# A second, modulated copy of the feed-forward operand in a row of 544 columns, read by 18 of 22 inner tiles

## The chip, the cores and the metric

The kernel runs on one core of one Trainium2 chip. The metric is the device time of one launch in microseconds (us). Times are medians over runs; one more execution is taken by the hardware profiler, and everything said below of single instructions is from that one.

## The reference

A two-layer diffusion backbone: 256 latent tokens `x` and 256 context tokens `y`, 1024 channels, 2816 inner channels in each feed-forward. Layer 0 mixes by differential attention, layer 1 by a Fourier transform; each mixer stands between two half-step SwiGLU feed-forwards. Every sub-layer normalizes, multiplies by a norm gain and a scale, and adds a shift.

```python
def modulate(h, shift, scale):
    return h * (1 + scale) + shift
def swiglu(h, w_gu, w_d):
    g, u = jnp.split(h @ w_gu, 2, axis=-1)
    return (jax.nn.silu(g) * u) @ w_d
...
x = x + 0.5 * mx[2] * swiglu(modulate(rms_norm(x, norm_g[i, 0]), mx[0], mx[1]), ffn1_w_gu[i], ffn1_w_d[i])
...   # attention (layer 0) or Fourier mixing (layer 1)
x = x + 0.5 * mx[8] * swiglu(modulate(rms_norm(x, norm_g[i, 2]), mx[6], mx[7]), ffn2_w_gu[i], ffn2_w_d[i])
```

The context tokens are needed only up to the attention of layer 0. So there is one feed-forward over 512 columns (layer 0, the first) and three over the 256 latent columns (layer 0 the second, layer 1 the first and the second). These three are called the **later feed-forwards** below, L0f1, L1f0 and L1f1.

## The kernel before, in words

**Products.** Everything is float32, and each product is made of three TensorE matmuls (`mm3`, L140): each operand is split into a rounded `hi` and a rest `lo`, and hi·hi, hi·lo and lo·hi are summed in PSUM. The first operand of a matmul (128 columns of weights) stays in the array, the second (256, 258 or 512 token columns of `xop_hi`, `xop_lo`) moves through it.

**Weights.** `unit` (L130) takes a weight tile of 1 MB by DMA from the SP queue into a ring of raw buffers and splits it in four pieces: ScalarE casts (`whi`, L101), VectorE subtracts (`wlo`, L102). In the later feed-forwards the rings of `whi` and `wlo` hold three tiles each (2 and 1 from `more_buffers`). So the cast of tile j + 3 can start only when the matmuls of tile j have ended.

**A later feed-forward.** `ffn` (L340) goes through the 22 inner tiles in two halves of 11. For each, `gate_up` (L301) runs 2 parts x 8 channel tiles x 3 = 48 matmuls into one PSUM tile `gu` out of a pool `psA` of **two**. So tile j + 2 can begin only when the evacuation of tile j has read its PSUM. The operand is not yet modulated: `scaled` (L294) writes x times the scale, without rstd (which is not known before the whole sum of squares is) and without the shift; the shift goes through the same weights as two extra columns (`scaled_shift`, L290), which makes 258. The evacuation puts both back: ScalarE copies the shift's product (`shw`, L317), VectorE multiplies both parts by rstd into `gus` (L319, which frees the PSUM tile), ScalarE takes Silu (L320), VectorE makes the product `hh` (L321), and `split` (L322) makes `h_hi` and `h_lo` of it. After each half, eight output tiles `dn` (`down`, L324) of 33 matmuls of 256 columns follow.

**Beside it.** The layers' scale, shift and gate vectors come from a large matrix by VectorE products with `junk` outputs (L197), `step(ROOM1)` (L347) placing some of them between the tiles, each with its own raw buffer and DMA. `modulated` (L280) makes an operand with rstd and shift in it: per channel tile VectorE `hmod` (L284), ScalarE `xop_hi` (L285) and VectorE `xop_lo` (L286). Before, only the attention uses it.

**Order.** Each engine works through its own list in order. The lists are made by the tile framework's scheduler, which places an operation when its modelled time and priority come up; `tc.high_priority(offset=URGENT)` moves an operation up by 200, `unit` moves weights up by `AHEAD = 60`.

Of the kernel before, what the change touches and what calls it, by code (L numbers as in the profile page):

```python
# [75 lines left out]
def tile_kernel(ctx: ExitStack, tc, xyT, small, rows, tables, w_mod0, w_mod, w_gu, w_d0, w_d, w_qkv, w_o, w_f, out):  # L76
# [196 lines left out]

    SX, SY = slice(0, NT), slice(NT, 2 * NT)

    gap(const, 416, "xop")
    xop_hi = const.tile([P, KT, 2 * NT], F32R, name="xop_hi")
    xop_lo = const.tile([P, KT, 2 * NT], F32R, name="xop_lo")

    def modulated(layer, w, s, r, dt):  # L280
        sl = (SX, SY)[s]
        h = work.tile([P, 512], F32, tag="hh", name="hmod")
        sh = mod[:, layer, s, 3 * w, dt:dt + 1]
        V.scalar_tensor_tensor(h[:, :NT], xy[:, dt, sl], amul[:, layer, s, w, dt:dt + 1], r, op0=ALU.mult, op1=ALU.mult)  # L284
        S.activation(xop_hi[:, dt, sl], h[:, :NT], AF.Identity, bias=sh)  # L285
        V.scalar_tensor_tensor(xop_lo[:, dt, sl], h[:, :NT], sh, xop_hi[:, dt, sl].bitcast(F32),  # L286
                               op0=ALU.add, op1=ALU.subtract)


    def scaled_shift(layer, w):  # L290
        sh = mod[:, layer, 0, 3 * w].unsqueeze(2).to_broadcast([P, KT, 2])
        split(xop_hi[:, :, NT:NT + 2], xop_lo[:, :, NT:NT + 2], sh)

    def scaled(layer, w, dt):  # L294
        a = amul[:, layer, 0, w, dt:dt + 1]
        S.activation(xop_hi[:, dt, :NT], xy[:, dt, :NT], AF.Copy, scale=a)
        V.scalar_tensor_tensor(xop_lo[:, dt, :NT], xy[:, dt, :NT], a, xop_hi[:, dt, :NT].bitcast(F32),  # L297
                               op0=ALU.mult, op1=ALU.subtract)


    def gate_up(layer, f, j, n, rstd, h_hi, h_lo, jj, fpool):  # L301
        nn = n if rstd is None else NT + 2
        hi, lo = (layer == f == 0 and early.pop(j, None)) or unit(w_gu[layer, f, j], 2048, f"gu{layer}{f}{j}")
        ps = pA(f"gu_{layer}_{f}_{j}")
        for part in range(2):
            for k in range(KT):
                c = k * 256 + part * P
                mm3(ps[:, part, :nn], hi[:, c:c + P], lo[:, c:c + P], xop_hi[:, k, :nn], xop_lo[:, k, :nn],
                    k == 0, k == KT - 1)
# [12 lines left out]
        split(h_hi[:, jj, :], h_lo[:, jj, :], h[:, :n])  # L322
# [17 lines left out]
    def ffn(layer, f, rstd, fpool, after, step):  # L340
        for half in range(2):
            h_hi = fpool.tile([P, JH, NT], F32R, tag="h_hi", name=f"h_hi_{layer}_{f}_{half}")
            h_lo = fpool.tile([P, JH, NT], F32R, tag="h_lo", name=f"h_lo_{layer}_{f}_{half}")
            for jj in range(JH):
                gate_up(layer, f, half * JH + jj, NT, rstd, h_hi, h_lo, jj, fpool)
                if f == 0 or half * JH + jj >= ADA_FROM:
                    step(ROOM1)  # L347
            for dt in range(KT):
                hi, lo = unit(w_d[layer * 2 + f - 1, half, dt], JH * P, f"d{layer}{f}{half}{dt}")
                down(layer, f, dt, SX, hi, lo, 0, h_hi, h_lo, JH, None, half == 1)  # L350
                if half == 1:
                    after(dt)
                step(ROOM1)
# [18 lines left out]
    nlam = const.tile([P, 1], F32, name="nlam")  # L372
    sgl = const.tile([P, 1], F32, name="sgl")
    rt = const.tile([P, 2, 2, 2, HD], F32, name="rt")
    gap(const, 96, "weights")

    def attention_tables():
        tb = rings["raw"].tile("tb")
# [30 lines left out]
    with tc.tile_pool(name="start", bufs=1) as spool, more_buffers("x0", **MORE0):  # L409
        def finish(dt):  # L410
            with tc.high_priority(offset=URGENT):
                first_columns(dt, begun[dt])
                h = work.tile([P, 512], F32, tag="hh", name="hmod")
                for s, sl in enumerate((SX, SY)):
                    a, sh = amul[:, 0, s, 0, dt:dt + 1], mod[:, 0, s, 0, dt:dt + 1]
                    V.tensor_scalar(h[:, sl], xr[:, dt, sl], a, sh, op0=ALU.mult, op1=ALU.add)
                split(xop_hi[:, dt], xop_lo[:, dt], h)

        xr = spool.tile([P, KT, 2 * NT], F32, name="xr")
        rstd0 = spool.tile([P, 2 * NT], F32, name="rstd0")  # L420
# [24 lines left out]

    acc = new_acc("l0a")
    with more_buffers("x1", **MORE1), tc.tile_pool(name="f00", bufs=1) as fpool:
        gap(fpool, 32, "h00")
        def beside0():
            yield from ada_steps(apool_, [(0, m, 2) for m in (2, 3, 4)] + [(0, 5, 1)], conds)  # L450
            attention_tables()
# [4 lines left out]
        for i, (a, b) in enumerate(SLICES):  # L456
# [9 lines left out]
            for u in range(4):  # L466
                cols = 2 * cnt * P
                src = w_d0[u, 2 * P * a * P:2 * P * b * P].rearrange("(p c) -> p c", p=P)
                units.append(unit(src, cols, f"d0{i}{u}"))

                if last and u == 2:
                    continue
                for sl in ((SY, SX) if last and u == 3 else (slice(0, 2 * NT),)):
                    for uu in ((2, 3) if last and u == 3 else (u,)):
                        hi, lo = units[uu]
                        for d2 in range(2):
                            dt = 2 * uu + d2
                            down(0, 0, dt, sl, hi, lo, d2 * cnt * P, h_hi, h_lo, cnt, pA if sl is SX else None, last)
                            if last:
                                with tc.high_priority(offset=URGENT):  # L480
                                    sumsq(acc, dt, sl)
                    if last and u == 3:
                        r1 = finish_rstd(acc, sl, f"l0a{sl.start}")
                        with tc.high_priority(offset=URGENT):
                            for dt in range(KT):
                                modulated(0, 1, sl.start // NT, r1, dt)
                if not last:
                    steps(ROOM_D0)
        steps.rest()
# [4 lines left out]
    with tc.tile_pool(name="att", bufs=1) as ap1, tc.tile_pool(name="att2", bufs=2) as ap2:  # L494
        gap(ap1, 32, "on")
        def project(c, toks, evac):

            hi, lo = unit(w_qkv[c], 2048, f"qkv{c}")
            for b in range(len(toks) // 2):
                ps = pC(f"pj_{c}{b}").rearrange("p (t n) -> p t n", t=2)  # L500
                for i in range(2):
                    t = toks[2 * b + i]
                    tsl = slice(t * P, (t + 1) * P)
                    for k in range(KT):
                        wh, wl = hi[:, k * 256:(k + 1) * 256], lo[:, k * 256:(k + 1) * 256]
                        xh, xl = xop_hi[:, k, tsl], xop_lo[:, k, tsl]
# [285 lines left out]
    with tc.tile_pool(name="fou", bufs=1) as fp:  # L792
# [129 lines left out]
```

## Time and profile before

| what | value |
|---|---|
| median of 3 runs (lowest, highest) | 1246.99 us (1244.59, 1247.35) |
| the profiled execution, its time and its span | 1248.06 us, 1246.3 us |
| PE (TensorE matmuls), busy | 1228.2 us, 99%, 8540 matmuls |
| DVE (VectorE), busy | 906.9 us, 73% |
| ACT (ScalarE), busy | 549.1 us, 44% |
| POOL (GpSimd), busy | 101.7 us, 8% |

PE's busy time counts a matmul from its start to its modelled end, and neighbouring ones overlap; so 99% says that PE nearly always has work, not that it can go no faster. What a matmul costs in a stream is the distance from one start to the next. "PEclk" is the share of TensorE's full clock that was granted in a stretch. In brackets behind a row of the timeline stands how long its engine had idled before it, and which instruction ended that.

### The profile page before, as it was taken

The page shows a single profiled execution, that of the slowest core. Times are in us where ns is not written, and L with a number is a line of the kernel's source. Part 1 is how long each engine was busy: PE and PEld are TensorE (multiplying, and loading weights), DVE is VectorE, ACT ScalarE, POOL GpSimd, SP SyncE. Part 2 cuts the span into 40 slices and gives each one's busy share as a digit, 9 for nine tenths or more (in the row PEclk, how much of TensorE's full clock was granted, in tenths as well). Part 3 has the DMA queues.
Part 4 walks back from the last instruction along what each step waited for, and adds up shares of the span by engine and source line. Part 5 has one row for each costly group of instructions (what it writes and reads, how often), then busy time and mean ns, then how long its engine had stood idle before and what let it go on. Part 6 is the DMA issues. An engine that isn't in the chain of part 4 may idle for free. (4 is left out here: it accounts for less than half of the span.)

```text
span 1246.3 us, 21263 instructions
## 1 busy us (share of the span) xinstructions
PE 1228.2 (99%) x8540; PEld 1118.9 (90%) x8540; DVE 906.9 (73%) x1768; ACT 549.1 (44%) x1207; POOL 101.7 (8%) x89
## 2 busy tenths in 40 slices
PE   8999999999999999999999999999999999999998
PEld 4688888888788989998899999999999999999998
DVE  1896985648993877876787788788698767666664
ACT  2332222232232535545555455555445545544552
POOL 0200000000000352340010000110000011000000
PEclk8999999999999899999989999999999999999999
DMA  9555464538891222121465686677586554536532
GB/s 362 217 219 187 169 251 136 217 132 319 303 349 57 102 102 102 35 97 42 169 220 207 237 303 231 223 280 248 191 322 240 184 195 170 192 120 248 188 119 81
DMA packets 37811, 241.94 MB, mean 194 GB/s; under 512 B 4224, under 2 KB 5376, under 8 KB 14672
## 3 DMA queue, kind: packets, MB, share of 16 engines
q1 hardware_dynamic: 37584, 240.25, 53.0%
q8 instruction: 67, 1.10, 0.3%
q0 software_dynamic: 128, 0.33, 0.2%
q14 instruction: 32, 0.26, 0.1%
HBM read 239.51 MB, written 1.05 MB: 193 GB/s over the span
## 5 line engine op out<-in xcount | busy, mean ns | idle before, releaser
L142 PE MATMUL gu<-xop_lo,whi_gu 128*128 128x258 f32 (+1 forms) x1408 | 439.0, 312 | 1.9 <-DVE xop_lo L297 1.9
L141 PE MATMUL gu<-xop_hi,whi_gu 128*128 128x258 f32 (+1 forms) x1408 | 438.4, 312 | 1.8 <-ACT whi_gu L101 1.5
L143 PE MATMUL gu<-xop_hi,wlo_gu 128*128 128x258 f32 (+1 forms) x1408 | 437.5, 311 | 0.2 <-DVE wlo_gu L102 0.2
L142 PEld LDWEIGHTS gu<-xop_lo,whi_gu 128*128 128x128 f32 x1408 | 265.6, 189 | 19.2 <-DVE xop_lo L297 2.6
L141 PEld LDWEIGHTS gu<-xop_hi,whi_gu 128*128 128x128 f32 x1408 | 265.6, 189 | 18.3 <-ACT whi_gu L101 1.7
L143 PEld LDWEIGHTS gu<-xop_hi,wlo_gu 128*128 128x128 f32 x1408 | 265.8, 189 | 17.0 <-DVE wlo_gu L102 0.6
L101 ACT CAST whi_gu<-raw_gu 128x512 fp32r<-128x512 f32 x352 | 194.7, 618 | 189.5 <-PE gu L142 106.3
L102 DVE TENSOR_TENSOR wlo_gu<-raw_gu,whi_gu 128x512 fp32r<-128x512 f32 x352 | 226.3, 690 | 56.8 <-ACT whi_gu L101 56.1
L143 PE MATMUL dn<-h_hi,wlo_d 128*128 128x256 f32 (+1 forms) x724 | 219.6, 305 | 0.0
L142 PE MATMUL dn<-h_lo,whi_d 128*128 128x256 f32 (+1 forms) x724 | 219.2, 304 | 0.0
L141 PE MATMUL dn<-h_hi,whi_d 128*128 128x256 f32 (+1 forms) x724 | 217.7, 304 | 0.3 <-DVE xy L336 0.3
L197 DVE SCALAR_TENSOR_TENSOR junk<-raw_m,cond_x 128x1024 f32<-128x1024 f32 x128 | 156.9, 1226 | 34.2 <-DMA raw_m<-in_w_mod 33.0
L101 ACT CAST whi_d<-raw_d 128x352 fp32r<-128x352 f32 (+2 forms) x256 | 105.9, 484 | 166.5 <-PE gu L142 84.8
L102 DVE TENSOR_TENSOR wlo_d<-raw_d,whi_d 128x352 fp32r<-128x352 f32 (+2 forms) x256 | 121.2, 527 | 59.0 <-ACT whi_d L101 59.0
L141 PEld LDWEIGHTS dn<-h_hi,whi_d 128*128 128x128 f32 x724 | 135.5, 188 | 7.8 <-PE dn L143 0.7
L142 PEld LDWEIGHTS dn<-h_lo,whi_d 128*128 128x128 f32 x724 | 136.0, 188 | 7.2
L143 PEld LDWEIGHTS dn<-h_hi,wlo_d 128*128 128x128 f32 x724 | 135.9, 188 | 7.2
L507 PE MATMUL pj<-whi_qkv,xop_hi 128*128 128x256 f32 x320 | 92.9, 290 | 0.8 <-DVE kr L553 0.8
L336 DVE SCALAR_TENSOR_TENSOR xy<-dn,mod,xy 128x256 f32<-128x256 f32 x112 | 50.5, 480 | 58.5 <-PE dn L143 58.2
L508 PE MATMUL pj<-wlo_qkv,xop_hi 128*128 128x256 f32 x320 | 92.0, 288 | 0.9 <-DVE wlo_qkv L102 0.8
L509 PE MATMUL pj<-whi_qkv,xop_lo 128*128 128x256 f32 x320 | 92.3, 289 | 0.2 <-DVE xop_lo L286 0.2
L101 ACT CAST h_hi<-hh 128x256 fp32r<-128x256 f32 (+1 forms) x88 | 40.4, 460 | 94.7 <-DVE hh L321 60.3
(225 smaller groups left out, 1418.1 us busy)
## 6 DMA issues: line engine op xcount, KB each, us to landing
raw_gu<-in_w_gu SPq DMA_DIRECT2D x88, 1024.0 KB, 5.0
raw_m<-in_w_mod SPq DMA_DIRECT2D x72, 1024.0 KB, 5.3
raw_d<-in_w_d SPq DMA_DIRECT2D x48, 704.0 KB, 4.1
raw_qkv<-in_w_qkv SPq DMA_DIRECT2D x12, 1024.0 KB, 4.7
raw_d<-in_w_d SPq DMA_DIRECT2D x8, 768.0 KB, 4.2
raw_d<-in_w_d SPq DMA_DIRECT2D x8, 640.0 KB, 4.8
raw_wo<-in_w_o SPq DMA_DIRECT2D x4, 1024.0 KB, 4.8
raw_wf<-in_w_f SPq DMA_DIRECT2D x4, 1024.0 KB, 6.8
```

The costliest lines, as they stand in the source:

```text
L101: S.copy(hi, src)
L102: V.tensor_sub(lo, src, hi.bitcast(F32))
L141: PE.matmul(ps, sh, mh, start=start, stop=False)
L142: PE.matmul(ps, sh, ml, start=False, stop=False)
L143: PE.matmul(ps, sl, mh, start=False, stop=stop)
L197: V.scalar_tensor_tensor(junk, w, 1.0, c, op0=ALU.mult, op1=ALU.mult, accum_out=out_col)
L336: V.scalar_tensor_tensor(xy[:, dt, so], ps[:, so.start - sl.start:so.stop - sl.start], mod[:, layer, s, 6 * f + 2, dt:dt + 1], xy[:, dt, s ...
L507: PE.matmul(ps[:, i], xh, wh, start=k == 0, stop=False)
L508: PE.matmul(ps[:, i], xh, wl, start=False, stop=False)
L509: PE.matmul(ps[:, i], xl, wh, start=False, stop=k == KT - 1)
```

## The change

The operand's rows grow from 512 to 544 columns. The unmodulated operand, the attention's and the Fourier stage's move to column `XA = 16`; columns `XB = 280` to 536 hold a second copy, with rstd and shift in it, which `modulated` makes at the start of each later feed-forward, under `URGENT`: 8 x (`hmod`, `xop_hi`, `xop_lo`). Inner tiles 0 to 3 (`DIRECT = 4`) still take the 258 unmodulated columns; tiles 4 to 21 take 256 columns of the copy and are evacuated as in the first feed-forward: Silu from PSUM, then one product from PSUM.

```diff
+XW = 544
+XA = 16
+XB = 280
+DIRECT = 4
...
-    gap(const, 416, "xop")
-    xop_hi = const.tile([P, KT, 2 * NT], F32R, name="xop_hi")
-    xop_lo = const.tile([P, KT, 2 * NT], F32R, name="xop_lo")
+    gap(const, 64, "xop")
+    xop_hi = const.tile([P, KT, XW], F32R, name="xop_hi")
+    xop_lo = const.tile([P, KT, XW], F32R, name="xop_lo")
...
-    def modulated(layer, w, s, r, dt):
+    def modulated(layer, w, s, r, dt, c0):
         sl = (SX, SY)[s]
+        xc = slice(c0, c0 + NT)
         h = work.tile([P, 512], F32, tag="hh", name="hmod")
...
-        S.activation(xop_hi[:, dt, sl], h[:, :NT], AF.Identity, bias=sh)
-        V.scalar_tensor_tensor(xop_lo[:, dt, sl], h[:, :NT], sh, xop_hi[:, dt, sl].bitcast(F32),
+        S.activation(xop_hi[:, dt, xc], h[:, :NT], AF.Identity, bias=sh)
+        V.scalar_tensor_tensor(xop_lo[:, dt, xc], h[:, :NT], sh, xop_hi[:, dt, xc].bitcast(F32),
                                op0=ALU.add, op1=ALU.subtract)
...
     def gate_up(layer, f, j, n, rstd, h_hi, h_lo, jj, fpool):
-        nn = n if rstd is None else NT + 2
+        if layer == f == 0:
+            c0, nn, rstd = 0, n, None
+        elif j < DIRECT:
+            c0, nn = XA, NT + 2
+        else:
+            c0, nn, rstd = XB, NT, None
+        xc = slice(c0, c0 + nn)
...
-                mm3(ps[:, part, :nn], hi[:, c:c + P], lo[:, c:c + P], xop_hi[:, k, :nn], xop_lo[:, k, :nn],
+                mm3(ps[:, part, :nn], hi[:, c:c + P], lo[:, c:c + P], xop_hi[:, k, xc], xop_lo[:, k, xc],
...
             for jj in range(JH):
+                if half == jj == 0:
+                    with tc.high_priority(offset=URGENT):
+                        for dt in range(KT):
+                            modulated(layer, 2 * f, 0, rstd, dt, XB)
                 gate_up(layer, f, half * JH + jj, NT, rstd, h_hi, h_lo, jj, fpool)
...
-    gap(const, 96, "weights")
+    gap(const, 64, "weights")
...
-        gap(fpool, 32, "h00")
...
-                                modulated(0, 1, sl.start // NT, r1, dt)
+                                modulated(0, 1, sl.start // NT, r1, dt, XA + sl.start)
...
-                    tsl = slice(t * P, (t + 1) * P)
+                    tsl = slice(XA + t * P, XA + (t + 1) * P)
```

Rows, gaps and columns together move where a matmul's operands start within 64 bytes (moving operand, weights), counted over all matmuls of the two built programs:

| matmuls | before | after |
|---|---|---|
| later feed-forwards, gate and up | 3168 of 258 columns at (0, 32) | 576 of 258 at (32, 32), 2592 of 256 at (0, 32) |
| first feed-forward, gate and up, 512 columns | 1056 at (0, 32) | 1056 at (32, 32) |
| first feed-forward, down, 512 columns | 468 at (0, 32) | 468 at (32, 32) |
| down, 256 columns | 1704 at (0, 32) | 1584 at (0, 32), 120 at (32, 32) |
| attention's projections `pj`, 256 columns | 960 at (32, 0) | 960 at (32, 32) |
| scores `s`, 512 columns | at (0, 0) | at (0, 0) |
| Fourier's weights `wf`, 256 columns | 192 at (32, 32) | 192 at (32, 32) |

The scheduler places the rest of VectorE's work otherwise, too. Three places follow. In a name like `wlo_gu016` the digits are layer, feed-forward and inner tile; `gu_0_1_2` is the PSUM tile of layer 0, feed-forward 1, inner tile 2. Lines are those of each program: L102, L197, L319 and L321 before are L108, L203, L333 and L335 after.

First place, VectorE in L0f1 around the evacuation `gus` of inner tile 2. Before:

```order
L102 TENSOR_TENSOR wlo_gu015_6006<-raw_gu015_6003,whi_gu015_6005 128x512 x2
L319 TENSOR_TENSOR gus_5848<-gu_0_1_2_5795,rstd_l0f1_5636 128x512
L102 TENSOR_TENSOR wlo_gu015_6006<-raw_gu015_6003,whi_gu015_6005 128x512 x2
L197 SCALAR_TENSOR_TENSOR junk_6218,mcols_1_3_5996<-raw_m131_6216,cond_x_102 128x1024
L321 SCALAR_TENSOR_TENSOR hh_5845<-gus_5848,shw_5846,sg_5844 128x256
L197 SCALAR_TENSOR_TENSOR junk_6220,mcols_1_3_5996<-raw_m131_6216,cond_x_102 128x1024
L102 TENSOR_TENSOR wlo_gu016_6077<-raw_gu016_6074,whi_gu016_6076 128x512 x2
L319 TENSOR_TENSOR gus_5919<-gu_0_1_3_5866,rstd_l0f1_5636 128x512
```

After:

```order
L203 SCALAR_TENSOR_TENSOR junk_6232,mcols_1_3_6022<-raw_m131_6230,cond_x_102 128x1024
L291 SCALAR_TENSOR_TENSOR hmod_5663<-xy_86,amul_99,rstd_l0f1_5634 128x256
L291 SCALAR_TENSOR_TENSOR hmod_5667<-xy_86,amul_99,rstd_l0f1_5634 128x256
L108 TENSOR_TENSOR wlo_gu016_6099<-raw_gu016_6096,whi_gu016_6098 128x512
L203 SCALAR_TENSOR_TENSOR junk_6234,mcols_1_3_6022<-raw_m131_6230,cond_x_102 128x1024
L108 TENSOR_TENSOR wlo_gu016_6099<-raw_gu016_6096,whi_gu016_6098 128x512 x3
L108 TENSOR_TENSOR xop_lo_106<-mod_98,xop_hi_105 128x8x2
L293 SCALAR_TENSOR_TENSOR xop_lo_106<-hmod_5663,mod_98,xop_hi_105 128x256
L293 SCALAR_TENSOR_TENSOR xop_lo_106<-hmod_5667,mod_98,xop_hi_105 128x256
L335 SCALAR_TENSOR_TENSOR hh_5733<-gus_5736,shw_5734,sg_5732 128x256
L335 SCALAR_TENSOR_TENSOR hh_5804<-gus_5807,shw_5805,sg_5803 128x256
L333 TENSOR_TENSOR gus_5878<-gu_0_1_2_5825,rstd_l0f1_5634 128x512
```

The `gus` of tile 2 stood between the pieces of tile 5's weights; now it stands behind all four pieces of tile 6's weights, a `junk`, and the pieces of the copy.

Second place, VectorE at the start of L1f0, around the `gus` of inner tile 0. Before:

```order
L255 TENSOR_SCALAR nv_l1f0_8080<-ss_l1f0_8075 128x2
L102 TENSOR_TENSOR wlo_gu103_8315<-raw_gu103_8312,whi_gu103_8314 128x512 x4
L319 TENSOR_TENSOR gus_8157<-gu_1_0_0_8104,rstd_l1f0_8087 128x512
L197 SCALAR_TENSOR_TENSOR junk_8527,mcols_1_6_8305<-raw_m161_8525,cond_x_102 128x1024
L102 TENSOR_TENSOR wlo_gu104_8386<-raw_gu104_8383,whi_gu104_8385 128x512 x2
```

After:

```order
L261 TENSOR_SCALAR nv_l1f0_8038<-ss_l1f0_8033 128x2
L108 TENSOR_TENSOR wlo_gu103_8305<-raw_gu103_8302,whi_gu103_8304 128x512 x3
L203 SCALAR_TENSOR_TENSOR junk_8509,mcols_1_6_8295<-raw_m161_8507,cond_x_102 128x1024
L108 TENSOR_TENSOR wlo_gu103_8305<-raw_gu103_8302,whi_gu103_8304 128x512
L291 SCALAR_TENSOR_TENSOR hmod_8050<-xy_86,amul_99,rstd_l1f0_8045 128x256
L291 SCALAR_TENSOR_TENSOR hmod_8054<-xy_86,amul_99,rstd_l1f0_8045 128x256
L333 TENSOR_TENSOR gus_8147<-gu_1_0_0_8094,rstd_l1f0_8045 128x512
```

A `junk`, which waits for its own DMA, and two `hmod` came ahead of the `gus` of tile 0.

Third place, VectorE in L1f1 around the `gus` of inner tile 2. Before:

```order
L102 TENSOR_TENSOR wlo_gu115_11445<-raw_gu115_11442,whi_gu115_11444 128x512 x2
L319 TENSOR_TENSOR gus_11294<-gu_1_1_2_11241,rstd_l1f1_11083 128x512
L102 TENSOR_TENSOR wlo_gu115_11445<-raw_gu115_11442,whi_gu115_11444 128x512 x2
L321 SCALAR_TENSOR_TENSOR hh_11291<-gus_11294,shw_11292,sg_11290 128x256
L102 TENSOR_TENSOR h_lo_1_1_0_11086<-hh_11291,h_hi_1_1_0_11085 128x256
```

After:

```order
L335 SCALAR_TENSOR_TENSOR hh_11099<-gus_11102,shw_11100,sg_11098 128x256
L108 TENSOR_TENSOR wlo_gu116_11458<-raw_gu116_11455,whi_gu116_11457 128x512
L335 SCALAR_TENSOR_TENSOR hh_11170<-gus_11173,shw_11171,sg_11169 128x256
L333 TENSOR_TENSOR gus_11244<-gu_1_1_2_11191,rstd_l1f1_11001 128x512
L108 TENSOR_TENSOR wlo_gu116_11458<-raw_gu116_11455,whi_gu116_11457 128x512 x2
```

Here one piece of tile 6's weights and two `hh` stand ahead of the `gus` of tile 2.

## Rows read from the trace of the kernel before

**Rows 1.** The page's first part: busy time, share, instructions of each engine.

```profile
PE 1228.2 (99%) x8540; PEld 1118.9 (90%) x8540; DVE 906.9 (73%) x1768; ACT 549.1 (44%) x1207; POOL 101.7 (8%) x89
```

**Rows 2.** Timeline of PE, ends of five unbroken stretches: start, us, line, operation, out<-in.

```profile
656.45 0.28 PE L141 MATMUL gu<-xop_hi,whi_gu 128*128 128x258 f32 x1
...
679.37 0.28 PE L143 MATMUL gu<-xop_hi,wlo_gu 128*128 128x258 f32 x1
...
710.26 0.28 PE L141 MATMUL dn<-h_hi,whi_d 128*128 128x256 f32 x1
...
717.96 0.28 PE L141 MATMUL dn<-h_hi,whi_d 128*128 128x256 f32 x1
...
1219.29 0.28 PE L141 MATMUL dn<-h_hi,whi_d 128*128 128x256 f32 x1
...
1238.72 0.28 PE L141 MATMUL dn<-h_hi,whi_d 128*128 128x256 f32 x1
...
1040.40 0.28 PE L141 MATMUL wf<-f_hi,whi_wf 128*128 128x256 f32 x1
...
1049.04 0.28 PE L141 MATMUL wf<-f_hi,whi_wf 128*128 128x256 f32 x1
...
475.03 0.29 PE L509 MATMUL pj<-whi_qkv,xop_lo 128*128 128x256 f32 x1
...
481.92 0.28 PE L507 MATMUL pj<-whi_qkv,xop_hi 128*128 128x256 f32 x1
```

**Rows 3.** Timeline of PE: 512-column matmuls, first and last of a stretch; two score pairs.

```profile
94.25 0.39 PE L141 MATMUL gu<-xop_hi,whi_gu 128*128 128x512 f32 x1
...
105.45 0.39 PE L141 MATMUL gu<-xop_hi,whi_gu 128*128 128x512 f32 x1
...
471.62 0.39 PE L603 MATMUL s<-k_lo,q_hi 64*128 64x512 f32 x2
471.85 0.40 PE L603 MATMUL s<-k_hi,q_lo 64*128 64x512 f32 x2
```

**Rows 4.** Timeline of ACT and DVE in L0f1 around the end of inner tile 3.

```profile
650.77 1.14 ACT L101 CAST whi_gu<-raw_gu 128x512 fp32r<-128x512 f32 x2 [2.66 <-PE gu L142]
...
645.66 1.30 DVE L102 TENSOR_TENSOR wlo_gu<-raw_gu,whi_gu 128x512 fp32r<-128x512 f32 x2 [0.20 <-ACT whi_gu L101]
646.87 0.69 DVE L319 TENSOR_TENSOR gus<-gu,rstd_l0f 128x512 f32<-128x512 f32 x1
...
648.67 1.23 DVE L197 SCALAR_TENSOR_TENSOR junk<-raw_m,cond_x 128x1024 f32<-128x1024 f32 x1
...
649.82 0.49 DVE L321 SCALAR_TENSOR_TENSOR hh<-gus,shw,sg 128x256 f32<-128x256 f32 x1
```

**Rows 5.** Timeline in L1f0 and L1f1: a junk's wait, two matmuls' wait for `gus`.

```profile
832.05 1.23 DVE L197 SCALAR_TENSOR_TENSOR junk<-raw_m,cond_x 128x1024 f32<-128x1024 f32 x1 [1.55 <-DMA raw_m<-in_w_mod]
...
830.55 0.39 PE L141 MATMUL gu<-xop_hi,whi_gu 128*128 128x258 f32 x1 [0.16 <-DVE gus L319]
...
1065.11 0.39 PE L141 MATMUL gu<-xop_hi,whi_gu 128*128 128x258 f32 x1 [0.15 <-DVE gus L319]
```

**Rows 6.** Windows: length, busy time (count) PE, PEld, DVE, ACT, POOL, PEclk, DMA.

```profile
619.00:622.60 3.60, 1.76 (x13) 1.35 (x11) 3.60 (x7) 3.60 (x10) 1.80 (x2) 1.00 0.73 269
622.60:629.50 6.90, 6.04 (x26) 5.58 (x26) 6.90 (x12) 4.14 (x11) 3.85 (x4) 0.51 0.48 167
...
816.00:831.00 15.00, 13.86 (x113) 13.36 (x112) 11.71 (x21) 6.67 (x16) 2.71 (x2) 1.00 0.84 309
```

**Rows 7.** Timeline of PE ahead of and within the stretch at half clock.

```profile
621.90 0.38 PE L141 MATMUL gu<-xop_hi,whi_gu 128*128 128x258 f32 x1 [1.53 <-ACT whi_gu L101]
623.19 0.58 PE L142 MATMUL gu<-xop_lo,whi_gu 128*128 128x258 f32 x1 [0.91 <-DVE xop_lo L297]
...
627.66 0.42 PE L143 MATMUL gu<-xop_hi,wlo_gu 128*128 128x258 f32 x1
...
629.16 0.42 PE L141 MATMUL gu<-xop_hi,whi_gu 128*128 128x258 f32 x1
```

More of the change, by code (lines that the diff above doesn't have):

```diff
@@ L291, in scaled_shift @@
         sh = mod[:, layer, 0, 3 * w].unsqueeze(2).to_broadcast([P, KT, 2])
-        split(xop_hi[:, :, NT:NT + 2], xop_lo[:, :, NT:NT + 2], sh)
+        split(xop_hi[:, :, XA + NT:XA + NT + 2], xop_lo[:, :, XA + NT:XA + NT + 2], sh)
     def scaled(layer, w, dt):
         a = amul[:, layer, 0, w, dt:dt + 1]
-        S.activation(xop_hi[:, dt, :NT], xy[:, dt, :NT], AF.Copy, scale=a)
-        V.scalar_tensor_tensor(xop_lo[:, dt, :NT], xy[:, dt, :NT], a, xop_hi[:, dt, :NT].bitcast(F32),
+        xc = slice(XA, XA + NT)
+        S.activation(xop_hi[:, dt, xc], xy[:, dt, :NT], AF.Copy, scale=a)
+        V.scalar_tensor_tensor(xop_lo[:, dt, xc], xy[:, dt, :NT], a, xop_hi[:, dt, xc].bitcast(F32),
                                op0=ALU.mult, op1=ALU.subtract)
     def gate_up(layer, f, j, n, rstd, h_hi, h_lo, jj, fpool):
-        nn = n if rstd is None else NT + 2
+        if layer == f == 0:
[5 more added lines that the diff above has]
+        xc = slice(c0, c0 + nn)
         hi, lo = (layer == f == 0 and early.pop(j, None)) or unit(w_gu[layer, f, j], 2048, f"gu{layer}{f}{j}")
@@ L416, in finish @@
                     V.tensor_scalar(h[:, sl], xr[:, dt, sl], a, sh, op0=ALU.mult, op1=ALU.add)
-                split(xop_hi[:, dt], xop_lo[:, dt], h)
+                split(xop_hi[:, dt, :2 * NT], xop_lo[:, dt, :2 * NT], h)
         xr = spool.tile([P, KT, 2 * NT], F32, name="xr")
@@ L800, in tile_kernel @@
                 ps = (pB, pC)[t](f"z{g}{t}")
-                tsl = slice(t * P, (t + 1) * P)
+                tsl = slice(XA + t * P, XA + (t + 1) * P)
                 for kk in range(2):
```

## Prediction, written before the changed kernel was run

> **What bounds the kernel now.** I read the busy times first. PE holds matmuls for 99% of the span [rows 1], so the time is the number of matmuls times their pitch (the distance from start to start), plus the few places where PE waits. The other engines cost something only where PE waits for them. VectorE is nevertheless the one to watch, with 73% on average and more in the feed-forwards.
>
> Next the pitch, from the timeline of PE in stretches where nothing waits; the reader is to divide the distance by the count [rows 2]. Gate and up, 258 columns: 656.45 to 679.37 is 22.92 us in 191 steps (192 rows), **120.0 ns**. Down, 256 columns, with the same address phases (0, 32): 7.70 us in 66 steps (67 rows) is **116.7 ns**, and 19.43 us in 165 steps (166 rows) is **117.8 ns**. `wf`, 256 columns at (32, 32): 8.64 us in 72 steps, **120.0 ns**. `pj`, 256 columns at (32, 0): 6.89 us in 58 steps (59 rows), **118.8 ns**. So two columns fewer are worth 2.2 to 3.3 ns, but 256 columns with both operands at 32 cost as much as 258.
>
> Third, who waits for whom around one inner tile of a later feed-forward. Its 48 matmuls take 48 x 0.120 = 5.76 us. The cast of tile 6's weights begins at 650.77, when tile 3's matmuls have ended and set its buffer free, after 2.66 us of idle ScalarE [rows 4]. The `gus` of tile 2, which frees the PSUM tile that tile 4 needs, was at 646.87, about 4 us ahead of that. This slack keeps PE going. At the start of L1f0 and of L1f1 there is none: there a tile's first matmul waited 0.16 and 0.15 us for `gus` [rows 5].
>
> **The change part by part.**
>
> *Narrower matmuls.* 3 x 18 x 48 = 2592 matmuls go from 258 to 256 columns at unchanged phases (0, 32). I price them at 117.0 ns, between the two down stretches, nearer the lower, since both share its phases: 2592 x 3.0 ns = **-7.8 us**. Bounds: 117.8 ns gives -5.7, 116.7 gives -8.6, an unchanged pitch 0.
>
> The nearest row for a price by column is the 258-column pitch itself, 120.0 / 258 = 0.465 ns, which would give 2592 x 0.93 ns = -2.4; the down rows speak for the larger step. The Trainium skill ("TensorE: Matmul & The Clock Gate", section "Back-to-back issue gap") speaks against this change: for a single warm matmul it gives a gap of N / 2.4 + 2.5 ns. An estimate from that page is 0.83 ns for two columns, 2.2 us in all instead of 7.8, with the total then near 1265.8. By the same formula 258 columns would take 110.0 ns; this trace shows 120.0, so formula and trace do not agree.
>
> *Other phases.* `pj` goes to (32, 32): 960 x (120.0 - 118.8) = **+1.2**. 120 down matmuls go to (32, 32): 120 x 3.3 ns = **+0.4**. The 576 remaining matmuls of 258 columns go to (32, 32), which no row shows for that width: 0 taken, bounds 576 x 3 ns = 1.7 either way. The 1524 matmuls of 512 columns go from (0, 32) to (32, 32). Before, their pitch is 11.20 us / 48 steps = 233.3 ns [rows 3]; the score pairs, both operands at the same phase 0, follow each other in 0.23 us [rows 3]. So I take 0. Bounds: 1524 x 3.3 ns = 5.0 in either direction if the step of the 256-column matmuls applies once, and 10.2 if twice.
>
> *The copy.* 3 x 8 channel tiles x 2 VectorE operations; the `hh` row has their kind and shape, 0.49 us [rows 4]: 7.8 us in each later feed-forward. VectorE was busy 11.71 of 15.00 us ahead of and in L1f0 [rows 6]: 1.26 us idle in a tile's 5.76, 5.0 in four tiles, in which the copy has to be ready. It does not fit: 2.8 us too much. ScalarE's eight `xop_hi` find room (6.67 of 15.00 busy) and I cost them at nothing. Tiles 4 to 21 lose `gus` (0.69 each) on VectorE and `shw` on ScalarE; PE does not wait for these in mid-stream, so their gain is 0, too. It would count if VectorE were late there.
>
> *The order around the copy*, the largest term. In **L0f1** the `gus` of tile 2 now stands behind all of tile 6's weights. These cannot begin until tile 3 has ended, and then tile 4 cannot begin until this `gus` is done. PE has nothing else to do. The chain from tile 3's last matmul, all prices from [rows 4]: one cast 0.57, one `wlo` 0.60 (two take 645.66 to 646.87), `junk` 1.15 (648.67 to 649.82), three `wlo` 1.81, two `xop_lo` and two `hh` at 0.49, 1.96, `gus` 0.69: 6.8. With the small split of the two shift columns in it I take **+7.0**. Bounds: 6.4 if the four small ones overlap to 0.40 each; 8.5 if the `junk` waits for its DMA as one did for 1.55 us [rows 5].
>
> In **L1f0** a `junk` and two `hmod` precede the `gus` of tile 0, where PE had no slack: 1.15 + 0.98 = **+2.1** (bounds 1.0 if the `junk` fits ahead of the last weight piece's cast, 3.7 with the DMA's 1.55). Tile 4 waits for the 2.8 us that do not fit, in part: **+1.5** (0 to 2.8). In **L1f1** two `hmod` precede the `gus` of tile 0, too: **+1.0** (0 to 1.0). Then one piece of tile 6's weights and an `hh` stand ahead of the `gus` of tile 2: 0.57 + 0.60 + 0.49 + 0.69 = **+2.4** (2.0 to 3.5). Together 14.0, bounds about 10 and 19. Raw weights that arrive by SP's queue are held back by the same time, and catch up: their buffers come free in the same order, and PE is behind, not ahead.
>
> *The clock.* After PE idled for 1.53 and 0.91 us within 1.3 us [rows 7], the granted clock was 0.51 for 6.90 us [rows 6], the lower of the two levels, 1.2 GHz, and the pitch there 1.50 us / 7 steps = 214 ns [rows 7]. One such stretch loses 6.90 x (1 - 120 / 214) = 3.0 us. The 15 us from 816 on had 1.14 us without a matmul and full clock throughout [rows 6]. A wait of 7 us is above what went before a fall, those of 2.1 and 2.4 us are near it. I take two falls at 2.7 (part of one lies in the wait): **+5.4**, bounds 0 and 9.0.
>
> **Sum**, on the profiled execution's 1248.06 us: -7.8 + 1.2 + 0.4 + 14.0 + 5.4 = +13.2, 1261.3. That execution is 1.07 us above the median of the runs, so the forecast is 1260.2, rounded to **1260**.
>
> **The rivals.**
>
> *VectorE keeps up* (0.08). If the `gus` of tile 2 is done before tile 3 ends, and the `hmod`s of layer 1 fall into idle time, no wait arises and the narrower matmuls remain: 1246.99 - 7.8 + 1.6 = **1240.8**, faster. What decides is that one position: `gus` of tile 2 ahead of tile 6's first `wlo`. For it: VectorE has 27% idle in all. Against: engines take their lists in order, and the list has it behind.
>
> *Half the waits and no fall* (0.10). The waits come out near half because the first evacuations run late anyway and PE's start shifts: 1246.99 - 7.8 + 1.6 + 7.0 = **1247.8**, no change. Against: each wait is a chain that begins with a matmul's end.
>
> *The waits, but no fall of the clock* (0.17): 1260.2 - 5.4 = **1254.8**. For it: the waits have single long gaps, and the fall that rows show came after several.
>
> *512 columns dearer at (32, 32)* (0.10): 1260.2 + 5.0 = **1265.2**, or 1270.4 if twice. For it: `wf` against the down rows at 256 columns. Against: the score pairs.
>
> *The copy hardly cheaper* (0.07): the change does not do what it says, if the pitch goes by columns alone: 1260.2 + 5.4 = **1265.6**. The formula of the page named above would give nearly this. Against: the down rows.
>
> **How the numbers follow.** My forecast has 0.48. The range, 1249 to 1271, leaves out the case without waits, part of the case with half of them, and the far ends of the dearest ones. 0.2%, 2.5 us, is about what a measurement tells from no change. Faster, 0.10: the first rival and the lower end of the second. Same, 0.07: the rest of the second. Slower, 0.83: all others.
>
> **What would show it.** In L0f1, the first matmul of tile 4 has some 7 us of idle PE before it, released by `gus`; shorter ones of 1 to 3 us stand at tiles 2 and 4 of L1f0 and L1f1. PEclk falls after the first. The pitch of tiles 4 to 21 is 117 ns, that of tiles 0 to 3 about 120, 512 columns 233 as before. I am wrong if tile 4 of L0f1 starts right behind tile 3, if the 256-column pitch stays at 119 or more, or if the 512-column pitch moves by over 1 ns.

## The result, and the profile after

| what | before | changed |
|---|---|---|
| median (lowest to highest) of 6 runs each | 1247.17 us (1244.59 to 1247.84) | 1258.67 us (1252.88 to 1262.87) |
| ratio, 95% interval | | 1.0091 (1.0065 to 1.0118) |
| the profiled execution, its span | 1248.06, 1246.3 us | 1259.59, 1257.8 us |

The change costs about 11.5 us. The page's first part of the changed kernel, against [rows 1]: PE has the same 8540 matmuls, 4.5 us less of busy time and 97% instead of 99%. Its matmuls have become a little cheaper, and it waits.

```profile
PE 1223.7 (97%) x8540; PEld 1119.3 (89%) x8540; DVE 887.0 (71%) x1761; ACT 539.9 (43%) x1177; POOL 101.7 (8%) x89
```

Where it waits, the timeline of PE shows. The first two rows end inner tiles 2 and 3 of L0f1; the others begin L0f1 tile 4, L1f0 tiles 2 and 4, and L1f1 tiles 2 and 4.

```profile
640.34 0.28 PE L149 MATMUL gu<-xop_hi,wlo_gu 128*128 128x258 f32 x1
...
646.11 0.28 PE L149 MATMUL gu<-xop_hi,wlo_gu 128*128 128x258 f32 x1
653.81 0.55 PE L147 MATMUL gu<-xop_hi,whi_gu 128*128 128x256 f32 x1 [7.41 <-DVE gus L333]
...
837.80 0.36 PE L147 MATMUL gu<-xop_hi,whi_gu 128*128 128x258 f32 x1 [3.40 <-DVE gus L333]
...
851.64 0.36 PE L147 MATMUL gu<-xop_hi,whi_gu 128*128 128x256 f32 x1 [0.55 <-ACT whi_gu L107]
...
1074.04 0.39 PE L147 MATMUL gu<-xop_hi,whi_gu 128*128 128x258 f32 x1 [0.95 <-DVE gus L333]
...
1088.25 0.55 PE L147 MATMUL gu<-xop_hi,whi_gu 128*128 128x256 f32 x1 [2.40 <-DVE gus L333]
```

The brackets sum to 14.71 us; 0.31 of that stood there before [rows 5], so 14.4 are new. Four of the five end with `gus`.

The timeline of ACT and DVE shows what lies behind the longest, from the end of tile 3 at 646.11 on.

```profile
646.31 1.14 ACT L107 CAST whi_gu<-raw_gu 128x512 fp32r<-128x512 f32 x2 [2.62 <-PE gu L148]
...
646.96 0.88 DVE L291 SCALAR_TENSOR_TENSOR hmod<-xy,amul,rstd_l0f 128x256 f32<-128x256 f32 x2
647.75 0.69 DVE L108 TENSOR_TENSOR wlo_gu<-raw_gu,whi_gu 128x512 fp32r<-128x512 f32 x1
648.36 1.22 DVE L203 SCALAR_TENSOR_TENSOR junk<-raw_m,cond_x 128x1024 f32<-128x1024 f32 x1
...
649.50 1.89 DVE L108 TENSOR_TENSOR wlo_gu<-raw_gu,whi_gu 128x512 fp32r<-128x512 f32 x3
651.31 0.17 DVE L108 TENSOR_TENSOR xop_lo<-mod,xop_hi 128x16 fp32r<-128x16 f32 x1
651.39 0.87 DVE L293 SCALAR_TENSOR_TENSOR xop_lo<-hmod,mod,xop_hi 128x256 fp32r<-128x256 f32 x2
652.18 0.88 DVE L335 SCALAR_TENSOR_TENSOR hh<-gus,shw,sg 128x256 f32<-128x256 f32 x2
652.98 1.28 DVE L333 TENSOR_TENSOR gus<-gu,rstd_l0f 128x512 f32<-128x512 f32 x2
```

In [rows 4] the `gus` of tile 2 came at 646.87 and tile 6's cast only at 650.77. Here the cast comes first, at 646.31, and `gus`, the first of the two at 652.98, after everything that depends on the cast. VectorE is busy without a gap; it works on the wrong thing, since tile 2's last matmul began at 640.34 and its `gus` could have run some 12 us earlier.

The clock, in windows of the changed kernel (length, PE, PEld, DVE, ACT, POOL, PEclk, DMA). One stretch at half clock lies at the start of L0f1, where the kernel before had 6.90 us of it [rows 6]. Three are new; each begins during or within 1.2 us after one of the three longest waits.

```profile
617.00:627.40 10.40, 10.05 (x46) 9.47 (x46) 10.18 (x19) 3.29 (x9) 5.18 (x5) 0.51 0.57 199
651.20:658.10 6.90, 4.29 (x20) 4.32 (x21) 5.34 (x14) 2.62 (x6) 0.00 (x0) 0.51 0.70 287
838.90:842.40 3.50, 3.50 (x19) 3.50 (x19) 3.50 (x7) 0.51 (x1) 0.00 (x0) 0.51 1.01 412
1088.10:1091.60 3.50, 3.35 (x16) 3.38 (x17) 3.50 (x9) 1.43 (x4) 0.00 (x0) 0.51 0.13 19
```

Last the pitches, by first and last row of unbroken stretches of the changed kernel: gate and up of 512 columns (48 steps), down of 512 (144), projections (63), gate and up of 256 (240).

```profile
92.55 0.39 PE L147 MATMUL gu<-xop_hi,whi_gu 128*128 128x512 f32 x1
...
103.70 0.39 PE L147 MATMUL gu<-xop_hi,whi_gu 128*128 128x512 f32 x1
...
114.84 0.39 PE L147 MATMUL dn<-h_hi,whi_d 128*128 128x512 f32 x1
...
147.51 0.40 PE L147 MATMUL gu<-xop_hi,whi_gu 128*128 128x512 f32 x1
...
471.47 0.28 PE L524 MATMUL pj<-whi_qkv,xop_hi 128*128 128x256 f32 x1
...
478.61 0.28 PE L524 MATMUL pj<-whi_qkv,xop_hi 128*128 128x256 f32 x1
...
661.46 0.28 PE L147 MATMUL gu<-xop_hi,whi_gu 128*128 128x256 f32 x1
...
690.00 0.28 PE L147 MATMUL gu<-xop_hi,whi_gu 128*128 128x256 f32 x1
```

That is 232.3, 226.9, 113.3 and 118.9 ns. The same stretch of down before ran from 116.65 to 150.24 in 144 steps, 233.3 ns:

```profile
116.65 0.39 PE L141 MATMUL dn<-h_hi,whi_d 128*128 128x512 f32 x1
...
150.24 0.39 PE L141 MATMUL gu<-xop_hi,whi_gu 128*128 128x512 f32 x1
```

In the six runs of the changed kernel the clock granted over the whole span went from 0.992 (1252.88 us, the fastest) to 0.982 (1262.87 us, the slowest), so the stretches at half clock are not the same in each.

The down of the first feed-forward gained 6.4 ns and the projections up to 5.5 (118.8 in [rows 2]), while the matmuls that the change is about gained 1.1 (120.0 in [rows 2]).

### The profile page after: what moved, and what is told of

Same layout as the page of the kernel before. It is cut to its first block, busy times and chain, and to the rows that moved or that the text cites. A ratio compares the mean times of both kernels' runs of the same rounds, so it can differ in the third digit from the quotient of the medians.

```text
span 1257.8 us, 21294 instructions
## 1 busy us (share of the span) xinstructions
PE 1223.7 (97%) x8540; PEld 1119.3 (89%) x8540; DVE 887.0 (71%) x1761; ACT 539.9 (43%) x1177; POOL 101.7 (8%) x89
## 5 line engine op out<-in xcount | busy, mean ns | idle before, releaser
L147 PE MATMUL gu<-xop_hi,whi_gu 128*128 128x256 f32 (+2 forms) x1408 | 438.6, 312 | 16.3 <-DVE gus L333 14.2
L148 PE MATMUL gu<-xop_lo,whi_gu 128*128 128x256 f32 (+2 forms) x1408 | 443.7, 315 | 2.5 <-DVE xop_lo L305 2.3
L149 PE MATMUL gu<-xop_hi,wlo_gu 128*128 128x256 f32 (+2 forms) x1408 | 441.7, 314 | 0.2 <-DVE wlo_gu L108 0.2
L147 PEld LDWEIGHTS gu<-xop_hi,whi_gu 128*128 128x128 f32 x1408 | 270.5, 192 | 33.1 <-ACT h_hi L107 7.6
L108 DVE TENSOR_TENSOR wlo_gu<-raw_gu,whi_gu 128x512 fp32r<-128x512 f32 x352 | 227.5, 691 | 87.8 <-ACT whi_gu L107 87.4
L148 PEld LDWEIGHTS gu<-xop_lo,whi_gu 128*128 128x128 f32 x1408 | 269.0, 191 | 20.0 <-DVE xop_lo L305 3.1
L149 PEld LDWEIGHTS gu<-xop_hi,wlo_gu 128*128 128x128 f32 x1408 | 269.8, 192 | 15.7 <-DVE wlo_gu L108 0.6
L203 DVE SCALAR_TENSOR_TENSOR junk<-raw_m,cond_x 128x1024 f32<-128x1024 f32 x128 | 156.3, 1221 | 37.8 <-DMA raw_m<-in_w_mod 36.7
L108 DVE TENSOR_TENSOR wlo_d<-raw_d,whi_d 128x352 fp32r<-128x352 f32 (+2 forms) x256 | 121.4, 524 | 75.3 <-ACT whi_d L107 75.2
L524 PEld LDWEIGHTS pj<-whi_qkv,xop_hi 128*128 128x128 f32 x320 | 60.6, 189 | 5.7 <-issue 3.6
```

The costliest lines, as they stand in the source:

```text
L147: PE.matmul(ps, sh, mh, start=start, stop=False)
L148: PE.matmul(ps, sh, ml, start=False, stop=False)
L149: PE.matmul(ps, sl, mh, start=False, stop=stop)
L203: V.scalar_tensor_tensor(junk, w, 1.0, c, op0=ALU.mult, op1=ALU.mult, accum_out=out_col)
L524: PE.matmul(ps[:, i], xh, wh, start=k == 0, stop=False)
```

## The experiments

Two questions were open. Do the waits come from the place of the evacuation in VectorE's list, or from the copy itself? And do the other pitches come from the operands' starts? All times are medians, with the ratio to the kernel before, run beside it, and its 95% interval in brackets.

**e1: the addresses without the copy.**

```diff
-DIRECT = 4
+DIRECT = 22
...
-                if half == jj == 0:
-                    with tc.high_priority(offset=URGENT):
-                        for dt in range(KT):
-                            modulated(layer, 2 * f, 0, rstd, dt, XB)
```

> The changed kernel's addresses with no copy (DIRECT = 22, modulated not called): all later tiles take 258 unmodulated columns, the output is the same. Theory, addresses: the shorter pitches that the changed kernel shows in layer 0 come from where operands start and recur here: 512-column down 227 ns, projections 114 to 115, 512-column gate and up 232; no wait before the fifth tile of a later feed-forward. Against the kernel before: 468 x 6.3 + 960 x 3.1 + 1056 x 1.2 = 7.2 us less, 3168 x 0.3 + 120 x 2.9 = 1.3 us more: about 1241. Rival, the prediction's own terms for the addresses (projections and 120 down matmuls dearer, 512 columns unchanged): 1248.8.

Measured 1241.94 us (0.9957, 0.9944 to 0.9971). Down of 512 columns from 113.27 to 145.93 is 32.66 us / 144 = 226.8 ns, as in the changed kernel. The addresses alone make the kernel faster; the prediction's +1.2 for the projections had the wrong sign, and its 0 for 512 columns was wrong.

```profile
113.27 0.39 PE L147 MATMUL dn<-h_hi,whi_d 128*128 128x512 f32 x1
...
145.93 0.40 PE L147 MATMUL gu<-xop_hi,whi_gu 128*128 128x512 f32 x1
```

**e2: the copy spread over tiles 0 to 7.**

```diff
-DIRECT = 4
+DIRECT = 10
...
-                if half == jj == 0:
-                    with tc.high_priority(offset=URGENT):
-                        for dt in range(KT):
-                            modulated(layer, 2 * f, 0, rstd, dt, XB)
                 gate_up(layer, f, half * JH + jj, NT, rstd, h_hi, h_lo, jj, fpool)
+                if half == 0 and jj < KT:
+                    modulated(layer, 2 * f, 0, rstd, jj, XB)
```

> The change with the copy made one channel tile after each of the inner tiles 0 to 7, at ordinary priority instead of the raised one, and first read by tile 10 (DIRECT = 10). Theory, order: the waits come from where the evacuations stand in VectorE's list, not from VectorE's total work, which is nearly the same here. So the wait ahead of tile 4 of the second feed-forward of layer 0 (7.6 us) falls below 0.5, as do those ahead of tile 4 in layer 1; one of 2 to 3 us may stay ahead of tile 2 of layer 1's first. Time: e1's 1241 less 1728 x 1.1 ns = 1.9, plus 2 to 4: 1241 to 1244. Rival, load: the copy's 16 operations are too much for VectorE wherever they stand; waits of 5 us or more in all remain in each later feed-forward: 1252 or more.

Measured 1241.29 us (0.995, 0.9938 to 0.9962). VectorE does the same work for the copy, and no wait stands ahead of any tile 4. The one that is left over 1 us stands ahead of tile 2 of L1f0:

```profile
825.88 0.39 PE L147 MATMUL gu<-xop_hi,whi_gu 128*128 128x258 f32 x1 [1.30 <-DVE gus L333]
```

17.4 us lie between this kernel and the changed one, which has six tiles more per feed-forward on the copy. The rival, VectorE's load, falls. The edit changes both the place and the priority of the copy; which of them would be enough was not tested.

**e3: the change with the starts of before.**

```diff
-XA = 16
-XB = 280
+XA = 0
+XB = 272
...
-    gap(const, 64, "xop")
+    gap(const, 32, "xop")
...
-    gap(const, 64, "weights")
+    gap(const, 96, "weights")
...
+        gap(fpool, 32, "h00")
```

> The change's copy and order with the start addresses (within 64 bytes) of the kernel before in all stages: XA = 0, XB = 272, gaps chosen for it. Theory: the waits (about 15 us) and the falls of the clock (about 4.6) stay, the narrower matmuls bring 2592 x 1.1 = 2.9, and the gain in layer 0 from addresses (about 6 us) is gone: 1247.2 + 16.7 = 1264, over the changed kernel's 1258.7. Rival, addresses have no part in it: 1258 to 1259 as in the changed kernel.

Measured 1260.9 us (1.011, 1.0097 to 1.0123). The long wait is there, and the 256-column matmuls take 28.27 us / 240 = 117.8 ns, not 118.9. Within 64 bytes their start is 0 as in the change; within 128 it is 64 here and 0 there. Those 1.1 ns are 2.9 us, most of the distance to the 1264 expected.

```profile
655.27 0.55 PE L147 MATMUL gu<-xop_hi,whi_gu 128*128 128x256 f32 x1 [7.46 <-DVE gus L333]
...
663.28 0.28 PE L147 MATMUL gu<-xop_hi,whi_gu 128*128 128x256 f32 x1
...
691.55 0.28 PE L147 MATMUL gu<-xop_hi,whi_gu 128*128 128x256 f32 x1
```

**e4: the copy at column 288**, nothing else.

```diff
-XB = 280
+XB = 288
```

> The change with the copy at column 288 instead of 280, so that the 2592 narrower matmuls start at (32, 32) instead of (0, 32); nothing else moves. By the rows of the Fourier weights and the 120 down matmuls at (32, 32), 120.0 ns against 118.9: 2.9 us more, about 1261.5. By the rows of the 512-column down and the projections at (32, 32), 114 ns for 256 columns: 2592 x 4.9 = 12.7 less, about 1246.

Measured 1260.58 us (1.0109, 1.0092 to 1.0127), near the first guess, but not by its pitch: that was 118.9 ns in L0f1 and in tiles 12 to 20 of layer 1, and 117.8 in tiles 5 to 10 there (L1f1, 1092.81 to 1121.07: 28.26 us / 240). Neither price holds: one start cannot be priced by other matmuls that have it.

**e5: the copy made and not read**; the copy's lines stay.

```diff
-DIRECT = 4
+DIRECT = 22
```

> The change with DIRECT = 22: the copy is made at its place, but no tile reads it, all take the unmodulated operand. Theory, order: PE waits for the evacuation that stands behind the copy and behind tile 6's weights, not for the copy; so the wait of 7.6 us ahead of tile 4 in the second feed-forward of layer 0 stays although nothing needs the copy, about 2.6 stays ahead of tile 4 of layer 1's second, and by the new list one of some 8 us stands ahead of tile 4 of layer 1's first. Time: e1's 1242 plus about 20 of waits plus 5 of clock: 1264 to 1270. Rival, PE waits for the copy: the waits at tile 4 are gone and only those of 1 to 3 us at tile 2 stay: 1246 or less.

Measured 1269.35 us (1.0179, 1.0165 to 1.0194), the slowest of all. PE's waits ahead of tile 4 of L0f1, L1f0 and L1f1, though nothing reads the copy:

```profile
650.15 0.55 PE L147 MATMUL gu<-xop_hi,whi_gu 128*128 128x258 f32 x1 [7.24 <-DVE gus L333]
...
854.27 0.55 PE L147 MATMUL gu<-xop_hi,whi_gu 128*128 128x258 f32 x1 [8.84 <-DVE gus L333]
...
1095.28 0.36 PE L147 MATMUL gu<-xop_hi,whi_gu 128*128 128x258 f32 x1 [2.40 <-DVE gus L333]
```

This settles the first question: PE waits for the evacuation behind the copy, not for the copy. Made without being read it costs 27.4 us over e1.

**e6: spread, and the copy at 64 within 128 bytes.**

```diff
-XW = 544
+XW = 576
-XB = 280
-DIRECT = 4
+XB = 296
+DIRECT = 11
...
+                if half == 0 and 1 <= jj < 1 + KT:
+                    modulated(layer, 2 * f, 0, rstd, jj - 1, XB)
-                if f == 0 or half * JH + jj >= ADA_FROM:
+                if half * JH + jj >= (2 if f == 0 else ADA_FROM):
```

> e2 with three edits: the copy's channel tiles follow inner tiles 1 to 8 and are read from tile 11 on; rows of 576 columns with the copy at 296, so that the narrower matmuls start at 64 within 128 bytes as those of 256-column down do and e3's copy did; in layer 1's first feed-forward the products beside it begin at tile 2. Theory: no wait over 1 us ahead of tile 2 or 4 in any later feed-forward; pitch of 256 columns 117.8 as in e3, not 118.9. Time: e1's 1242 less 1584 x 2.5 ns = 4.0: about 1238. Rival, the pitch of the narrower matmuls does not depend on the start: 118.9, 1240; rival, a wait stays in layer 1's first: 1241.

Measured 1238.83 us (0.994, 0.9922 to 0.9959). Tiles 12 to 20 of L0f1 take 44.80 us / 384 = 116.7 ns, the lower of the two pitches of the down matmuls [rows 2]; the same tiles of L1f0 take 117.8. A wait of 1.59 us for rstd is left in L1f0.

```profile
721.47 0.28 PE L147 MATMUL gu<-xop_hi,whi_gu 128*128 128x256 f32 x1
...
766.27 0.28 PE L147 MATMUL gu<-xop_hi,whi_gu 128*128 128x256 f32 x1
```

**e7: one start alone, the hidden operand's**, in the kernel before:

```diff
     with more_buffers("x1", **MORE1), tc.tile_pool(name="f00", bufs=1) as fpool:
-        gap(fpool, 32, "h00")
```

> The kernel before with one edit: the gap of 32 bytes ahead of the first feed-forward's hidden operand is taken out, so that its 468 down matmuls of 512 columns and 120 of 256 start at (32, 32) instead of (0, 32). Theory: 468 x 6.3 = 2.9 us less, 120 x 2.9 = 0.3 more: 2.6 less, 227 ns for 512 columns, all other pitches as before. Rival, the 227 ns need the other shifts, too: no change.

Measured 1246.3 us (0.9985, 0.9976 to 0.9994), 1.9 us less by the interval's middle. Down of 512 columns: 32.68 us / 144 = 226.9 ns. One gap of 32 bytes makes this pitch.

```profile
115.11 0.40 PE L141 MATMUL dn<-h_hi,whi_d 128*128 128x512 f32 x1
...
147.79 0.40 PE L141 MATMUL gu<-xop_hi,whi_gu 128*128 128x512 f32 x1
```

**e8: one start alone, the operand's**, in the kernel before:

```diff
-    gap(const, 416, "xop")
+    gap(const, 384, "xop")
...
-    gap(const, 96, "weights")
+    gap(const, 128, "weights")
```

> The kernel before with the operand alone shifted by 32 bytes (gaps 384 and 128 instead of 416 and 96): 512-column gate and up from (0, 32) to (32, 32) within 64 bytes, projections' first operand from 0 to 32. Theory: projections 114.8 instead of 117.9 ns, 960 x 3.1 = 3.0 us less; gate and up of 512 columns 1056 x 1.2 = 1.3 less; 258 columns 3168 x 0.3 = 0.9 more; 3.4 us less in all. Rival: the projections' gain needs the changed kernel's longer rows; less than 1 us.

Measured 1237.97 us (0.9924, 0.9912 to 0.9935), nearly three times the gain that was expected. Gate and up of 512 columns take 10.98 us / 48 = 228.8 ns and of 258 columns 28.57 us / 240 = 119.0 (233.3 and 120.0 before); the projections average 114.9 over their unbroken steps, as in the changed kernel. 1056 x 4.5 + 3168 x 1.0 + 960 x 3.0 = 10.8 us. The 1.2 ns expected for 512 columns came from another start: within 64 bytes the operand is at 32 in this kernel and in the changed one, within 128 at 96 here and at 32 there.

```profile
90.41 0.39 PE L141 MATMUL gu<-xop_hi,whi_gu 128*128 128x512 f32 x1
...
101.39 0.39 PE L141 MATMUL gu<-xop_hi,whi_gu 128*128 128x512 f32 x1
...
649.16 0.28 PE L141 MATMUL gu<-xop_hi,whi_gu 128*128 128x258 f32 x1
...
677.73 0.28 PE L141 MATMUL gu<-xop_hi,whi_gu 128*128 128x258 f32 x1
```

**e9: e7 and e8 together** in the kernel before, no copy.

```diff
-    gap(const, 416, "xop")
+    gap(const, 384, "xop")
...
-    gap(const, 96, "weights")
+    gap(const, 128, "weights")
...
-        gap(fpool, 32, "h00")
```

> The kernel before with e7's and e8's edits together, no copy. Theory, the two pitches are set by their own operands' starts and add: e8's 1238.0 less 468 x 6.3 ns = 2.9, plus 0.3 for 120 down matmuls: 1235.4; 229 and 119 ns for gate and up, 227 for 512-column down, 114.9 for the projections. Rival, they are not independent: no better than e8.

Measured 1236.29 us (0.9914, 0.9899 to 0.9929). Against e8 the intervals overlap. In its trace both pitches stand together (229.0 ns for gate and up of 512 columns, 227.1 for down, means of the unbroken steps); that the times add is likely but not shown.

**e10: e9's starts and e6's copy**, as edits of e6:

```diff
-XA = 16
-XB = 296
+XA = 0
+XB = 280
...
-    gap(const, 64, "xop")
+    gap(const, 384, "xop")
...
-    gap(const, 64, "weights")
+    gap(const, 128, "weights")
```

> e9's starts with e6's copy: rows of 576 columns, unmodulated operand at column 0, copy at 280 (64 within 128 bytes), made after inner tiles 1 to 8, read from tile 11 on. Theory: gate and up of 256 columns 117.0 ns as in e6 against 118.9 of 258 in e8: 1584 x 1.9 = 3.0 less than e9: 1232.4, if no new wait arises; with one of 1.7 us at the start of layer 1's first feed-forward, as in e6, 1234. Rival, the copy is not worth its work even without waits: e9's time or more.

Measured 1235.61 us (0.9913, 0.9893 to 0.9933). It is ahead of both kernels by some 11 and 23 us, yet not measurably ahead of e9. The copy's matmuls missed the 117.0 ns: they averaged 117.8 over the unbroken steps, and in L1f0 tiles 12 to 20 took 45.57 us / 384 = 118.7.

```profile
909.87 0.28 PE L147 MATMUL gu<-xop_hi,whi_gu 128*128 128x256 f32 x1
...
955.44 0.28 PE L147 MATMUL gu<-xop_hi,whi_gu 128*128 128x256 f32 x1
```

With its order mended and its start chosen the copy costs nothing that can be measured; that it brings anything here is not shown.

## Why the prediction was right

The time (1258.67 for 1260), the sign and the mechanism came out as forecast. The terms did so in part: the narrower matmuls were 4.9 us worse than forecast and the other starts 8.3 us better. That these two errors largely cancelled is luck, and the closeness of the sum owes much to it.

| term | forecast | measured |
|---|---|---|
| 2592 matmuls of 256 columns | -7.8 | 2592 x (118.9 - 120.0) = -2.9 |
| 576 matmuls of 258 columns | 0 | 576 x (120.3 - 120.0) = +0.2 |
| projections | +1.2 | 960 x (114.8 - 117.9), means of the unbroken steps, = -3.0 |
| 120 down matmuls | +0.4 | 120 x (119.9 - 116.7), means of the unbroken steps, = +0.4 |
| 512 columns, 1056 and 468 | 0 | 1056 x -1.0 - 468 x 6.4 = -4.1 |
| waits | +14.0 | +14.4 |
| clock | +5.4 | +5.0 behind the waits, +1.6 elsewhere |

The rows sum to 11.6 us; the two profiled executions lie 11.53 us apart.

**The order, the largest term, was right.** The chain in L0f1 ran as written down from [rows 4]: 7.41 us of wait where 7.0 stood, through the operations listed but for the first link: the first `wlo`, at 647.75, came behind two `hmod` that VectorE still had to do, not behind the cast. L1f0's tile 2 got 3.40 instead of 2.1: its `junk` waited 1.13 us for its DMA, which the bound of 3.7 held. Tile 4 of L1f0 had 0.55 instead of 1.5, and it waited for a cast, not for the copy: that VectorE's 2.8 us too much would fall on PE was the weak step. L1f1 gave 0.95 and 2.40 for 1.0 and 2.4. e2 and e5 show the cause from both sides.

**The clock** was near in size and wrong in count. Beside the long stretch after the 7.41 us, both the wait of 3.40 and that of 2.40 were followed by a short one of 3.5 us. The new ones cost 1.9 (tile 4 of L0f1, 661.46 - 653.81 less 48 x 118.9 ns = 5.71), 1.6 and 1.5 us, worked out in the same way: 5.0 together. The stretch at the start of L0f1, which grew from 6.9 to 10.4 us, cost 2.0 more (13.02 us from the second matmul of tile 0 to the first of tile 1, 11.06 before). That is not the copy's doing: e8 and e9, which make none, have 10.4 us at half clock there, too. A shorter stretch at the start of the projections gives back at most 0.4 (41 rows in 9.58 us before, in 9.15 after). Nor is a fall behind a short wait certain: in e4 the same wait of 2.40 us ahead of tile 4 of L1f1 was followed by none.

**The narrower matmuls were mis-sized.** The step that failed is "I price them at 117.0 ns [...] since both share its phases". They share the start within 64 bytes, not within 128: 64 for the down operand, 0 for the copy. At 64 the copy's matmuls took 117.8 (e3) and 116.7 (e6, L0f1), within the prediction's bounds; at 0, 118.9. The start is not the whole reason: at 64 they took 118.7 in L1f0 of e10. An estimate by the Trainium skill's formula ("TensorE: Matmul & The Clock Gate", section "Back-to-back issue gap"), 0.83 ns for two columns, came nearer to the measured 1.1 than my 3.0. The rival *The copy hardly cheaper* (0.07), with -2.4 us, had this term nearly right; its 1265.6 was missed because the other starts gained. The formula knows only the width, and the traces give 256 columns 113.3 to 120.0 ns by where they start.

**Other phases** were wrong in sign. The step was to price the projections at (32, 32) by `wf` at (32, 32), and to keep 512 columns unchanged because score pairs were. The 6.4 ns by which down of 512 columns moved are over the 1 ns that the prediction named as a sign of being wrong; the 118.9 stays just under its other sign, 119. e1, e7 and e8 show that each kind of matmul answers to its own starts. A rule that gives a pitch from a start was not found: e4 refutes two, and the start within 128 bytes does not settle it either. At 96, 258 columns took 120.3 in e1 (rows of 544 columns) and 119.0 in e8 (rows of 512). The row's length is not the reason by itself: with rows of 576 in both, they took 34.80 us / 288 = 120.8 in e6 and 34.17 / 288 = 118.6 in e10, in tiles 4 to 10 of L0f1.

## What to carry to other kernels

When a change adds work at the start of a stage, read the list of each engine for what now stands ahead of the operation that frees PE's buffer: an evacuation behind a conversion that waits for PE's own end makes a wait as long as everything between, even where the added work is off the path and has time. Spread such work, one piece behind each tile. Where a stream of matmuls is the bound, try paddings of 32 bytes ahead of its operands before restructuring: one shift of the operand (e8) gave 0.76%, more than the narrower matmuls could have; measure each, since a pitch at one start says little of other matmuls at that start.

## What was not expected of the hardware

**The pitch depends on the operands' starts, finely and without a plain rule.** 512 columns took 226.8 to 233.3 ns, 256 columns 113.3 to 120.0, with the same instructions. For 512 columns the runs sort by the moving operand's start within 128 bytes (means of the unbroken steps): down 233.3 at 64 (before, e3, e8) and 226.9 to 227.1 at 32 (the other nine kernels); gate and up 233.3 to 233.4 at 0 (before, e3, e7), 232.1 to 233.1 at 32 (six kernels) and 228.9 to 229.0 at 96 (e8, e9, e10).

**One program can hold two pitches.** In the profiled execution of e9, 258 columns from the same addresses take 34.28 us / 288 = 119.0 ns in tiles 4 to 10 of L0f1, 35.20 / 288 = 122.2 in tiles 4 to 10 of L1f0, and 45.71 / 384 = 119.0 in tiles 12 to 20 of the same feed-forward:

```profile
642.01 0.28 PE L141 MATMUL gu<-xop_hi,whi_gu 128*128 128x258 f32 x1
...
676.29 0.28 PE L141 MATMUL gu<-xop_hi,whi_gu 128*128 128x258 f32 x1
...
821.04 0.39 PE L141 MATMUL gu<-xop_hi,whi_gu 128*128 128x258 f32 x1 [0.19 <-DVE gus L319]
...
832.87 0.28 PE L141 MATMUL gu<-xop_hi,whi_gu 128*128 128x258 f32 x1
...
868.07 0.28 PE L141 MATMUL gu<-xop_hi,whi_gu 128*128 128x258 f32 x1
...
910.47 0.28 PE L141 MATMUL gu<-xop_hi,whi_gu 128*128 128x258 f32 x1
...
956.18 0.28 PE L141 MATMUL gu<-xop_hi,whi_gu 128*128 128x258 f32 x1
```

3.2 ns over the 288 steps are 0.9 us, and L1f1 shows the same. In both, the longer pitch begins at a short wait ahead of tile 2 (0.19 us in the row at 821.04, 0.18 in L1f1; tile 1 still took 118.7 and 118.9) and ends with tile 10, where down follows. But e8, with the same starts and the same two waits, took 118.7 behind them. What chooses the pitch stayed open. That profiled execution took 1240.55 us, the longest of e9's runs (1234.8 to 1240.55).
